# A trunk layer on one core: gate r's first two block products in the last head, a sixth pair of gate tiles, sums of tokens by eight additions

## The chip, the cores and the metric

One core of a Trainium2 chip runs the whole layer in one launch. The metric is the time of one execution in microseconds on the device; the median of several runs is what counts.

## The reference, cut to what matters

```python
u = _rmsnorm(h, norm1_g)                       # 512 tokens x 1024 channels, float32
a_glu, q, k, v, r, g_low, gate_a, gate_b = _split_cols(u @ w_in)
c = a_glu[..., :C] * sigmoid(a_glu[..., C:])
c = silu(_layernorm(_causal_dwconv(c, conv_dw_w, conv_dw_b), conv_ln_g, conv_ln_b))
y_conv = c @ w_conv_out
o = _gla_chunked(qh, kh, vh, gkh)              # 4 heads, chunks of 64 tokens
o = o * rsqrt(mean(o * o) + EPS) * gla_norm_g
y_gla = (o * silu(r)) @ w_gla_out
merged = sigmoid(gate_a) * y_conv + sigmoid(gate_b) * y_gla
h = h + merged @ w_o
u2 = _rmsnorm(h, norm2_g)
z = _causal_dwconv(u2 @ w_ffn_up, ffn_dw_w, ffn_dw_b)
h = h + (silu(z[..., :F]) * z[..., F:]) @ w_ffn_down
return _rmsnorm(h, final_g)
```

The batch is one sequence of 512 tokens; q and k have 512 columns, v, r, gate_a and gate_b have 1024 each, and F is 2816.

## The kernel before, in words

**Products.** All matrix products are held to float32 by splitting each operand into a rounded high part and the rest: three matmuls stand for one (`mm3`, lines 529 to 531: high x low, low x high, high x high). The activations are `uh`/`ul`, a weight tile (128 x 1024) is `whi`/`wlo`.

**Weights.** A list `order` fixes the sequence of the weight tiles. For each, SP issues the load into one of four `raw` buffers, ACT casts it to `whi` (line 414 or 444), and `wlo` comes in one of two ways: DVE subtracts (line 415 or 452), or, for the tiles in the set `ADDED`, ACT writes minus the weight (line 446) and POOL issues a DMA that adds the weight from memory again (line 447). There are four `whi` and four `wlo`, and a tile is prepared `LOOK` = 2 tiles ahead of its use. The program order that Python writes is each engine's order; engines wait for each other by semaphores.

**The work around the change, in PE's order.** The value weights, the convolution's inputs (`glu`), a low-rank decay, and then four heads of the linear attention, each with queries, keys, scores, states and outputs; a loop over `h` runs head `h` and the rest of head `h - 1` together, and in the gaps of a head stand `gate_b` tiles, one gate weight tile of eight k-steps and 24 matmuls of 512 columns. In the last round (h = 4) these are gate_b(2) to gate_b(5): ahead of the scores, ahead of the states, between states and outputs, and behind the outputs.

**Gate r** (`seven("w_r")`) comes next. It computes all of r with seven block products in place of eight, on 2 x 2 blocks of tokens and weights: the steps a11, a12, s1, n2, s4, n3, a22 in this order, each of two weight tiles (d = 0, 1) and 24 matmuls of 512 columns in all. a11, a12 and a22 read blocks of the activations as they are; s1, n2, s4 and n3 read sums of token blocks, which `token_sums_7` makes on DVE (passes of lines 1292 and 1305; high parts on ACT, line 1300). The weights of s1, n2 and a22 are running sums in `kept` (DVE, line 362), those of n3 are sums on POOL (line 373). Results go from PSUM banks (`x` in cv and one mm, `y` in mm, `z` in ax) to tiles `r`: `put_r` copies (ACT, line 1532), adds or subtracts (DVE, line 1539), takes the silu (ACT, line 1540) and multiplies into the head outputs `ot` (DVE, line 1546).

**Behind it** the products are transposed to channels (`gated_o`, PE line 1237, ACT line 1244, DVE line 1245), each group of four transposes into one of three ax banks: channel tiles 4 to 7 at step a22, 0 to 3 in the first pair. Then come the **pairs** of gate tiles (`pair_7`, `two_tiles`): two tiles of 1024 x 128 weights by the same seven products, here with the four weights x1, x3, x2, x4 and 84 matmuls of 256 columns, the weight sums on POOL (line 386). `MERGE` lists the pairs: gb (6, 7) and four of ga, with tiles of the output projections between and behind them. The output product w_o, the second norm, the FFN (up projection, short convolution, down projection by seven products, whose sums come from the same `token_sums_7`) and the last norm end the layer.

**Pacing.** The convolution runs on DVE as a chain of some 300 small passes (line 889), and the sums of tokens wait in a list `urgent` that is served ahead of it. Each call of `weight` hands out a share of it (`fill(share)`), so these passes are spread between the weights' own passes in DVE's order. Shares per tile are constants, as in

```python
        share = {"two": 2.5, "w_glu": RATE, "w_r": 2.0}.get(name, RATE)
        if name == "w_gb" and j > 3:
            share = 2.0 if j == 4 else 6.8
```

Of the kernel before, what the change touches and what calls it, by code (L numbers as in the profile page):

```python
# [10 lines left out]
F32 = mybir.dt.float32  # L11
# [23 lines left out]
AHEAD = 6  # L35

MERGE = [("w_gb", 6, 7), ("w_ga", 0, 1), ("w_ga", 2, 3), ("w_ga", 4, 5), ("w_ga", 6, 7)]
# [25 lines left out]
STEPS += [(step, d) for step in ("n2", "s4", "n3", "a22") for d in (0, 1)]  # L63
R_STEPS = [(step, d) for step in ("a11", "a12", "s1", "n2", "s4", "n3", "a22") for d in (0, 1)]
# [36 lines left out]
def trunk_layer(ctx: ExitStack, tc: tile.TileContext, a: dict, out: bass.AP):  # L101
# [300 lines left out]
    def split_weight(halves=False, between=None):  # L402

        if len(ready) < len(order):
# [4 lines left out]
            if name in SEVEN or name == "two":  # L409
# [5 lines left out]
                two_low[:] = [nc.vector.tensor_tensor(lo, raw, hi.bitcast(F32), ALU.subtract)]  # L415
# [54 lines left out]
    def weight(name, j, ahead=LOOK):  # L470
# [8 lines left out]
        if name == "w_gb" and j > 3:  # L479
            share = 2.0 if j == 4 else 6.8  # L480
# [783 lines left out]
    def token_sums_7(u, src, hi, lo):  # L1264
# [19 lines left out]
        def chain(step, start, *terms):  # L1284


            def one(first, op, x):
                if first:
                    work[step] = src[step]()
                begin = work[step] if not first else work[start] if isinstance(start, str) else [start]  # L1290
                for o, b, y in pieces(work[step], begin, [x]):
                    nc.vector.tensor_tensor(o, as_f32(b), f32(y), op)

            return [(1.7, lambda n=n, op=op, x=x: one(n == 0, op, x)) for n, (op, x) in enumerate(terms)]
# [75 lines left out]
    def quarters(pool, tag, bufs, halves=1, dt=F32R):  # L1370
# [11 lines left out]
        {"s1": x_src, "n2": h_src, "s4": b_src, "n3": b_src},  # L1382
# [5 lines left out]
    s1_n2, of_s1, s4, of_n2, of_s4, n3, of_n3 = merge_sums  # L1388
    heads = [Head(h) for h in range(HEADS)]
    for h in range(HEADS + 1):  # L1390
        old = heads[h - 1] if h else None
        new = heads[h] if h < HEADS else None
        if new:
            late_glu = glu(KT - LATE_GLU + h - 1) if h <= LATE_GLU else None
# [599 lines left out]
```

## Time and profile before

| | |
|---|---|
| median of 3 runs | 818.69 us (818.48 to 818.78) |
| the profiled execution | 820.03 us |
| its span in the profile | 818.3 us |
| granted clock, mean | 0.999 |
| PE busy | 808.6 us, 99% |
| DVE busy | 705.9 us, 86% |
| ACT busy | 488.9 us, 60% |
| POOL busy | 196.5 us, 24% |
| DMA | 113.60 MB, mean 139 GB/s |

How to read it. PE is TensorE, DVE is VectorE, ACT is ScalarE, POOL is GpSimd, SP issues loads. A row of a timeline gives the start, the duration, the engine, the source line, the operation, what it writes and reads, the shape, and how often it follows itself; a bracket at the end gives the engine's idle time ahead of it and what ended that. PE's matmuls overlap, so a matmul's duration is longer than the distance to the next one; the distance between starts tells what one costs. The span is what the profile covers; the execution's own time is 1.7 us longer.

### The profile page before, as it was taken

How to read it: one execution, taken by the hardware profiler on the slowest of the kernel's cores; microseconds unless marked ns; L12 is line 12 of the kernel's file. 1: busy time of each engine (PE TensorE's matmuls, PEld its weight loads, DVE VectorE, ACT ScalarE, POOL GpSimd, SP SyncE). 2: the span in 40 equal slices, each digit the busy share in tenths (PEclk: the TensorE clock that was granted, in tenths of full speed). 3: DMA queues.
4: the chain of work that ended last, by engine and by line, in shares of the span. 5: the costliest groups of instructions: out<-in, count | busy, mean ns of one | idle time of the engine just before them, and what ended most of it. 6: DMA issues, size and time to landing. Idle time of an engine off the chain costs nothing.

```text
span 818.3 us, 11468 instructions
## 1 busy us (share of the span) xinstructions
PE 808.6 (99%) x4227; PEld 695.4 (85%) x4227; DVE 705.9 (86%) x1105; ACT 488.9 (60%) x744; POOL 196.5 (24%) x176
## 2 busy tenths in 40 slices
PE   9999999999999999999999999999999999999996
PEld 8888888788888888989888898898889987899885
DVE  6879999998999878486789889989966999789895
ACT  6667788677547565394434645556445663366554
POOL 2025433332203332122001100230123311522012
PEclk9999999999999999999999999999999999999999
DMA  8488758645841232432558613156742446335662
GB/s 331 150 190 188 179 165 184 152 120 131 187 116 38 79 127 78 131 106 99 160 130 215 190 53 103 52 178 158 142 139 80 142 119 164 104 103 179 156 129 103
DMA packets 36472, 113.60 MB, mean 139 GB/s; under 512 B 3688, under 2 KB 8944, under 8 KB 36416
## 3 DMA queue, kind: packets, MB, share of 16 engines
q1 hardware_dynamic: 28912, 86.39, 30.9%
q0 software_dynamic: 7488, 26.48, 18.9%
q8 instruction: 33, 0.54, 0.3%
q14 instruction: 23, 0.19, 0.1%
q10 hardware_dynamic: 16, 0.00, 0.0%
HBM read 110.76 MB, written 2.10 MB: 138 GB/s over the span
## 4 chain that ended last, share of the span: by engine, by line
PE 85%; DVE 13%; issue 1%; ACT 1%; POOL 0%; POOLq 0%; ACTq 0%; DVEq 0%
PE mm L529 19%; PE mm L530 19%; PE mm L531 19%; DVE c L889 5%; PE cv L530 4%; PE cv L529 4%; PE cv L531 4%; DVE aside L889 3%; PE ax L531 2%; PE ax L529 2%; PE ax L530 2%; PE mm L743 2%; DVE wlo L415 1%; PE ax L1217 1%; PE cv L743 1%
## 5 line engine op out<-in xcount | busy, mean ns | idle before, releaser
L529 PE MATMUL mm<-uh,wlo 128*128 128x512 f32 (+1 forms) x532 | 193.9, 364 | 0.0
L530 PE MATMUL mm<-ul,whi 128*128 128x512 f32 (+1 forms) x532 | 191.5, 360 | 0.0
L531 PE MATMUL mm<-uh,whi 128*128 128x512 f32 (+1 forms) x532 | 191.5, 360 | 0.0
L415 DVE TENSOR_TENSOR wlo<-raw,whi 128x1024 fp32r<-128x1024 f32 x82 | 95.2, 1169 | 33.5 <-ACT whi L414 29.7
L386 POOL TENSOR_TENSOR raw<-raw,raw 128x512 f32<-128x512 f32 x39 | 60.0, 1539 | 240.1 <-DVE wlo L415 119.7
L529 PEld LDWEIGHTS mm<-uh,wlo 128*128 128x128 f32 x532 | 100.5, 189 | 15.3 <-DVE wlo L452 0.3
L531 PEld LDWEIGHTS mm<-uh,whi 128*128 128x128 f32 x532 | 100.4, 189 | 15.3
L530 PEld LDWEIGHTS mm<-ul,whi 128*128 128x128 f32 x532 | 100.5, 189 | 14.8
L414 ACT CAST whi<-raw 128x1024 fp32r<-128x1024 f32 x82 | 78.9, 966 | 39.0 <-PE mm L531 23.4
L444 ACT CAST whi<-raw 128x1024 fp32r<-128x1024 f32 x80 | 83.7, 1050 | 29.4 <-PE mm L531 13.2
L452 DVE TENSOR_TENSOR wlo<-raw,whi 128x1024 fp32r<-128x1024 f32 x50 | 66.8, 1342 | 7.4 <-ACT whi L444 7.1
L414 ACT CAST whi<-kept 128x1024 fp32r<-128x1024 f32 (+1 forms) x40 | 40.3, 1009 | 32.4 <-DVE kept L362 16.5
L415 DVE TENSOR_TENSOR wlo<-kept,whi 128x1024 fp32r<-128x1024 f32 (+1 forms) x40 | 48.8, 1221 | 7.6 <-ACT whi L414 7.5
L889 DVE SCALAR_TENSOR_TENSOR aside<-cv,pp,aside 128x255 f32<-128x255 f32 (+6 forms) x112 | 52.4, 468 | 0.0
L889 DVE SCALAR_TENSOR_TENSOR c<-aside,btmp,c 128x247 f32<-128x247 f32 (+13 forms) x93 | 52.3, 568 | 0.0
L889 DVE SCALAR_TENSOR_TENSOR c<-cv,pp,c 128x247 f32<-128x247 f32 (+13 forms) x93 | 43.4, 467 | 1.4 <-ACT c L885 1.4
L446 ACT ACTIVATE wlo<-raw 128x1024 fp32r<-128x1024 f32 x28 | 29.5, 1061 | 18.9 <-PE mm L529 18.9
L1336 ACT COPY tmp<-mm 128x256 f32<-128x256 f32 x38 | 14.1, 370 | 36.5 <-PE mm L531 35.9
L1718 DVE SCALAR_TENSOR_TENSOR tmp<-mm,pp,tmp 128x511 f32<-128x511 f32 (+1 forms) x42 | 31.0, 741 | 2.6 <-ACT tmp L1715 2.5
L1718 DVE SCALAR_TENSOR_TENSOR tmp<-tmp,pp,tmp 128x511 f32<-128x511 f32 (+1 forms) x32 | 27.8, 887 | 0.4
L1489 DVE TENSOR_TENSOR hres<-hres,mm 128x512 f32<-128x512 f32 (+1 forms) x37 | 24.6, 675 | 2.7 <-PE mm L531 1.9
L530 PE MATMUL cv<-ul,whi 128*128 128x512 f32 (+1 forms) x72 | 25.6, 356 | 0.0
(503 smaller groups left out, 2092.9 us busy)
## 6 DMA issues: line engine op xcount, KB each, us to landing
raw<-in_w_up_dram SPq DMA_DIRECT2D x44, 512.0 KB, 3.8
raw<-in_w_glu_dram SPq DMA_DIRECT2D x16, 512.0 KB, 5.0
raw<-in_w_down_dram SPq DMA_DIRECT2D x15, 512.0 KB, 4.3
wlo<-in_w_glu_dram POOLq DMA_DIRECT2D x12, 512.0 KB, 7.1
kept<-in_w_down_dram POOLq DMA_DIRECT2D x10, 512.0 KB, 6.1
raw<-in_w_v_dram SPq DMA_DIRECT2D x8, 512.0 KB, 5.4
raw<-in_w_qk_dram SPq DMA_DIRECT2D x8, 512.0 KB, 6.4
raw<-in_w_gb_dram SPq DMA_DIRECT2D x8, 512.0 KB, 4.3
```

The lines of the kernel that those rows point to most:

```text
L386: work = nc.gpsimd.tensor_tensor(out, x, y, ALU.add)
L414: nc.scalar.copy(hi, raw)
L415: two_low[:] = [nc.vector.tensor_tensor(lo, raw, hi.bitcast(F32), ALU.subtract)]
L444: nc.scalar.copy(hi, raw)
L446: pace[0] = nc.scalar.mul(lo, raw, -1.0)
L452: pace[0] = nc.vector.tensor_tensor(lo, raw, hi.bitcast(F32), ALU.subtract)
L529: nc.tensor.matmul(acc, ll, rh, start=first, stop=False, **kw)
L530: nc.tensor.matmul(acc, lh, rl, start=False, stop=False, **kw)
L531: nc.tensor.matmul(acc, lh, rh, start=False, stop=last, **kw)
L889: nc.vector.scalar_tensor_tensor(out[:, j:], x[:, : half_t - j], w, out[:, j:], ALU.mult, ALU.add)
L1489: done = nc.vector.tensor_tensor(hres[t, n][:, c], hres[t, n][:, c], acc[:, c], op)
L1718: nc.vector.scalar_tensor_tensor(z[:, s:], acc[:, : T - s], w[j], z[:, s:], ALU.mult, ALU.add)
```

## The change

Six edits go together.

1. **Sums of tokens** (`token_sums_7`) by eight additions in place of ten, through two shared sums k1 and k2. For the merge, the first three used to be computed near 31 to 39 us, and the rest in the heads; now all eight stand near the end of the last head, in `heap` buffers. The FFN's sums use the same function.
2. **Gate r** becomes a generator. Its a11 and a12 run in the last round's two slots of gate_b(4) and gate_b(5); s1 follows the heads. PSUM banks are taken when first used, and y and z change places.
3. **The low parts of a11's and a12's four weights** are made by ACT and two accumulating DMAs of POOL each, and no longer by DVE. The shares in the last round are 1.0 and 3.4 for these tiles.
4. **gate_b tiles 4 and 5** become a pair, the second of now six, behind the two w_gla tiles that follow the first, with no tile between its parts.
5. **Transposes**: channel tiles 4 and 5 at a22, then two behind each of x1, x3 and x2 of the first pair. Silu and product of two token tiles (from a12) move to n2.
6. **The FFN's list** of sums is regrouped for the eight additions.

The diff, cut to what the text speaks of:

```diff
 GROUPS = (((0, 2), (1, 3), (4, 6), (5, 7)), ((8, 10), (9, 11), (20, 21)), ((12, 14), (13, 15), (16, 18), (17, 19)))
-AHEAD = 6
-
-MERGE = [("w_gb", 6, 7), ("w_ga", 0, 1), ("w_ga", 2, 3), ("w_ga", 4, 5), ("w_ga", 6, 7)]
+AHEAD = 4
+
+MERGE = [("w_gb", 6, 7), ("w_gb", 4, 5), ("w_ga", 0, 1), ("w_ga", 2, 3), ("w_ga", 4, 5), ("w_ga", 6, 7)]
 R_PAIRS = ((0, 4), (1, 5), (2, 6), (3, 7))
 LATE_GLU = 2
 _HALVES = [("w_gla", 2 + h // 2, h % 2) for h in range(8)]
-BEHIND = [[], _HALVES[:4], _HALVES[4:8]]
+BEHIND = [[], [], _HALVES[:4], _HALVES[4:8]]
 BEHIND += [[("w_conv", m, half) for m in pair for half in range(2)] for pair in O_PAIRS[:2]]
 MERGE_REST = [("w_conv", m) for pair in O_PAIRS[2:] for m in pair]
-PLAIN_GLA = {0: (0, 1), 2: (6, 7)}
+PLAIN_GLA = {0: (0, 1), 3: (6, 7)}
 LOOK = 2
...
 STEPS = [("a11", 0), ("a11", 1), ("a12", 0), ("s1", 0), ("a12", 1), ("s1", 1)]
 STEPS += [(step, d) for step in ("n2", "s4", "n3", "a22") for d in (0, 1)]
+R_EARLY = {("a11", 0): 1.0, ("a11", 1): 1.0, ("a12", 0): 3.4, ("a12", 1): 3.4}
+R_ADDED = {("a11", 0), ("a11", 1), ("a12", 0), ("a12", 1)}
 R_STEPS = [(step, d) for step in ("a11", "a12", "s1", "n2", "s4", "n3", "a22") for d in (0, 1)]
 START = {ET.PE, ET.Activation, ET.DVE, ET.SP}
...
+                if name == "w_r" and spec[1:] in R_ADDED:
+                    two_low[:] = [nc.scalar.mul(lo, raw, -1.0)]
+                    src = block(name, spec[0], spec[2], *R_LOADS[spec[1]])
+                    for m in (slice(0, 2), slice(2, 4)):
+                        nc.gpsimd.dma_start(shaped(name, lo)[:, m], src[:, m], accum_op=ALU.add)
+                else:
+                    two_low[:] = [nc.vector.tensor_tensor(lo, raw, hi.bitcast(F32), ALU.subtract)]
                 with ExitStack() as order_of:
                     for ins in behind:
                         order_of.enter_context(tc.issue_after(ins.ins))
...
-            share = 2.0 if j == 4 else 6.8
+        if name == "w_r" and j[1:] in R_EARLY:
+            share = R_EARLY[j[1:]]
 
         fill(share + (1.75 if order[min(len(ready), len(order)) - 1] in ADDED else 0))
...
-
-
-            def one(first, op, x):
...
-
-            return [(1.7, lambda n=n, op=op, x=x: one(n == 0, op, x)) for n, (op, x) in enumerate(terms)]
+        def combine(step, l, op, r, over=None):
+
+            def at(x):
+                return work[x] if isinstance(x, str) else [x]
+
+            def one():
+                if step not in work:
+                    work[step] = work[over] if over else src[step]()
+                for o, x, y in pieces(work[step], at(l), at(r)):
+                    nc.vector.tensor_tensor(o, as_f32(x), as_f32(y), op)
...
         acts7 = {s: [[y[:, k, :] for k in range(4)] for y in x] for s, x in (("a11", a11), ("a12", a12), ("a22", a22))}
-        s1 = chain("s1", a21[0], (sub, a22[0]), (add, a21[1]), (sub, a22[1]))
-        n2 = chain("n2", "s1", (sub, a11[0]), (sub, a11[1]))
-        s4 = chain("s4", "n2", (add, a12[0]), (add, a12[1]))
-        n3 = chain("n3", a11[0], (sub, a21[0]), (add, a11[1]), (sub, a21[1]))
-        return acts7, [s1 + n2, split_sum("s1"), s4, split_sum("n2"), split_sum("s4"), n3, split_sum("n3")]
+        both = combine("k1", a11[0], add, a11[1]) + combine("k2", a21[0], add, a21[1])
+        n3 = combine("n3", "k1", sub, "k2")
+        s1 = combine("s1", "k2", sub, a22[0], "k2") + combine("s1", "s1", sub, a22[1])
+        n2 = combine("n2", "s1", sub, "k1", "k1")
+        s4 = combine("s4", "n2", add, a12[0]) + combine("s4", "s4", add, a12[1])
+        return acts7, [both + n3 + s1, split_sum("s1"), n2 + split_sum("n2"), s4 + split_sum("s4"), split_sum("n3")]
...
         {"s1": h_room, "n2": h_room, "s4": late_room, "n3": h_room},
     )
 
 
-    s1_n2, of_s1, s4, of_n2, of_s4, n3, of_n3 = merge_sums
...
-        bank = {"x": [mm_bank(), mm_bank()], "y": [mm_bank(), mm_bank()], "z": [ax_bank(), ax_bank()]}
+        y, z = (ax_bank, mm_bank) if name == "w_r" else (mm_bank, ax_bank)
+        take = {"x": mm_bank, "y": y, "z": z}
+        bank = {}
...
     rt, gated = {}, []
-    urgent += s4 + of_s4 + n3 + of_n3
-
     def sums_for(step):
         while urgent and step in ("s1", "n2", "s4", "n3") and step not in merge_acts:
             urgent.pop(0)[1]()
 
+    def multiply(t, n):
+        if (t, n) not in ((2, 0), (3, 0)):
+            nc.scalar.activation(rt[t, n], rt[t, n], AF.Silu)
+        nc.vector.tensor_tensor(ot[t, n], ot[t, n], rt[t, n], ALU.mult)
+
+    def multiply_all(done):
+        with tc.issue_after(done.ins) if done else ExitStack():
+            while gated:
+                multiply(*gated.pop(0))
+
     def put_r(step, t, n, acc):
         if step in ("a11", "s1", "n2"):
-            rt[t, n] = rp_.tile([P, T], F32, tag="r", name=nm("r"), bufs=6)
-            return nc.scalar.copy(rt[t, n], acc)
+            rt[t, n] = heap() if step == "a11" else rp_.tile([P, T], F32, tag="r", name=nm("r"), bufs=6)
+            done = nc.scalar.copy(rt[t, n], acc)
+            if step == "n2":
+                multiply_all(done)
+            return done
         if step == "a22":
             rt[t, n] = rp_.tile([P, T], F32, tag="r", name=nm("r"), bufs=6)
             nc.scalar.activation(rt[t, n], acc, AF.Silu)
...
-            nc.scalar.activation(r, r, AF.Silu)
         if step == "a22":
             done = None
-        with tc.issue_after(done.ins) if done else ExitStack():
-            while gated:
-                i, j = gated.pop()
-                nc.vector.tensor_tensor(ot[i, j], ot[i, j], rt[i, j], ALU.mult)
+        if step != "a12":
+            multiply_all(done)
         gated.append((t, n))
         if (step, t, n) == ("a22", 3, 0):
-            i, j = gated.pop()
-            nc.vector.tensor_tensor(ot[i, j], ot[i, j], rt[i, j], ALU.mult)
+            multiply(*gated.pop())
         return done if step == "n3" else None
 
     def r_at(step, i):
         if (step, i) == ("a22", 1):
-            for m in range(4, KT):
+            for m in range(4, 6):
...
+    r_work = seven("w_r", R_PAIRS, [ByTile(k) for k in range(4)], None, r_at, put=put_r, before=sums_for)
+    heads = [Head(h) for h in range(HEADS)]
+    for h in range(HEADS + 1):
+        old = heads[h - 1] if h else None
+        new = heads[h] if h < HEADS else None
+        if new:
+            late_glu = glu(KT - LATE_GLU + h - 1) if h <= LATE_GLU else None
+            new.decays()
+            new.queries()
+        else:
+            gate_b(2)
+        if old:
+            old.scores()
+        if not new:
+            urgent += n3_s1 + of_s1 + of_n2
+        new.keys() if new else gate_b(3)
+        if old:
+            old.states()
+            next(late_glu) if h <= LATE_GLU else gate_b(0) if new else next(r_work)
+            old.outputs()
+            next(late_glu) if h <= LATE_GLU else gate_b(1) if new else next(r_work)
+    behind += [roots_at[0]]
+    gla_scope.close()
+    late_scope, late = scoped("late", 1, "right")
+    r_scope, rp_ = scoped("r", 8, "right")
+    urgent += of_s4 + of_n3
+    for _ in r_work:
+        pass
     half_of = [range(KT // 2), range(KT // 2, KT)]
...
-            if n == 0 and j in (1, 2):
-                for m in range(2 * j - 2, 2 * j):
+            if n == 0 and j < 3:
+                for m in ((6, 7), (0, 1), (2, 3))[j]:
                     gated_o(m, ax_bank)
                 if j == 2:
                     start_norms()
-            if j == 0 or n >= 2:
+            if j == 0 or n >= 3:
...
             up_acts, sums = ffn_sums()
-            s1_n2, of_s1, s4, of_n2, of_s4, n3, of_n3 = sums
-            sums = [s1_n2, of_n2 + of_s1, s4 + n3, of_n3 + of_s4]
+            n3_s1, of_s1, of_n2, of_s4, of_n3 = sums
+            sums = [n3_s1[:3], n3_s1[3:] + of_n2[:1], of_n2[1:] + of_n3 + of_s1, of_s4]
```

What moves, as each engine's rows in program order. First **DVE in gate r**, the rows up to the low part of s4's second weight (the last row). Before; `kept` rows are running sums of weights, L1539 and L1546 drain r:

```order
L362 TENSOR_TENSOR kept_2078<-kept_2078,raw_2434 128x1024
L415 TENSOR_TENSOR wlo_2493<-kept_2153,whi_2492 128x1024
L1539 TENSOR_TENSOR r_2466<-ax_2428,r_2466 128x512
L362 TENSOR_TENSOR kept_2153<-kept_2153,raw_2446 128x1024
L1539 TENSOR_TENSOR r_2480<-ax_2429,r_2480 128x512
L1546 TENSOR_TENSOR h_1617<-h_1617,r_2466 128x512
L415 TENSOR_TENSOR wlo_2529<-kept_2078,whi_2528 128x1024
L362 TENSOR_TENSOR kept_2078<-kept_2078,kept_2582 128x1024
L415 TENSOR_TENSOR wlo_2538<-kept_2153,whi_2537 128x1024
L362 TENSOR_TENSOR kept_2153<-kept_2153,rx_2590 128x1024
L415 TENSOR_TENSOR wlo_2579<-raw_2434,whi_2578 128x1024
L415 TENSOR_TENSOR wlo_2587<-raw_2446,whi_2586 128x1024
```

And now (line numbers are up by 8; L1314 are low parts of token sums, L1538 drains, L1231 belongs to a head's norm):

```order
L1538 TENSOR_TENSOR h_2340<-cv_2411,h_2340 128x512
L1314 TENSOR_TENSOR sumsq_2469<-tmpq_2453,sumsq_2466 128x512
L1314 TENSOR_TENSOR sumsq_2469<-tmpq_2454,sumsq_2466 128x512
L1538 TENSOR_TENSOR h_2354<-mm_2412,h_2354 128x512
L423 TENSOR_TENSOR wlo_2448<-kept_1947,whi_2447 128x1024
L423 TENSOR_TENSOR wlo_2459<-kept_2019,whi_2458 128x1024
L1314 TENSOR_TENSOR hq_2511<-hq_2264,sumsq_2508 128x512
L1314 TENSOR_TENSOR hq_2512<-hq_2265,sumsq_2508 128x512
L364 TENSOR_TENSOR kept_1947<-kept_1947,kept_2506 128x1024
L423 TENSOR_TENSOR wlo_2503<-raw_2312,whi_2502 128x1024
L364 TENSOR_TENSOR kept_2019<-kept_2019,rx_2519 128x1024
L423 TENSOR_TENSOR wlo_2516<-raw_2322,whi_2515 128x1024
```

The twelve rows held five wlo (the first of s1, then n2 and s4), four `kept` sums and three passes on r and h. Now they hold the four wlo of n2 and s4, two `kept` sums, the two drains of a12 and four low parts of token sums; s1's wlo and the other `kept` sums stand ahead of them, and the product on h stands behind.

Second, **POOL's queue over the last head and gate r**. Before: one accumulating DMA for each gate tile, two tiny norm operations (rstd), then the weight sums of n3:

```order
L447 DMA wlo_2149<-in_w_gb_dram 128x1024
L447 DMA wlo_2194<-in_w_gb_dram 128x1024
L581 TENSOR_TENSOR rstd_2138<-mean_2136,mhalf 128x4
L447 DMA wlo_2252<-in_w_gb_dram 128x1024
L581 TENSOR_TENSOR rstd_2365<-mean_2363,mhalf 128x4
L373 TENSOR_TENSOR raw_2312<-raw_2312,raw_2434 128x512 x2
L373 TENSOR_TENSOR raw_2375<-raw_2375,raw_2446 128x512 x2
```

And now; `wlo_2249` is a11's second weight, `wlo_2307` and `wlo_2317` are a12's:

```order
L455 DMA wlo_2149<-in_w_gb_dram 128x1024
L421 DMA wlo_2194<-in_w_r_dram 128x2x256 x2
L589 TENSOR_TENSOR rstd_2138<-mean_2136,mhalf 128x4
L421 DMA wlo_2249<-in_w_r_dram 128x2x256 x2
L421 DMA wlo_2307<-in_w_r_dram 128x2x256 x2
L421 DMA wlo_2317<-in_w_r_dram 128x2x256 x2
L589 TENSOR_TENSOR rstd_2376<-mean_2374,mhalf 128x4
L375 TENSOR_TENSOR raw_2199<-raw_2199,raw_2312 128x512 x2
L375 TENSOR_TENSOR raw_2254<-raw_2254,raw_2322 128x512 x2
```

gate_b(4) and gate_b(5) had one issue each; r's four weights have two each, three of them between the two rstd.

Third, **PE at the end of a22**: the last transpose of the third group, eight matmuls of the first pair, and the fourth group (`ax_2769`), before:

```order
L1237 MATMUL ax_2760<-ident,h_2146 128x128
L529 MATMUL mm_2782<-uh_97,wlo_2703 128x256
L530 MATMUL mm_2782<-ul_98,whi_2702 128x256
L531 MATMUL mm_2782<-uh_97,whi_2702 128x256
L529 MATMUL mm_2782<-uh_97,wlo_2703 128x256
L530 MATMUL mm_2782<-ul_98,whi_2702 128x256
L531 MATMUL mm_2782<-uh_97,whi_2702 128x256
L529 MATMUL mm_2782<-uh_97,wlo_2703 128x256
L530 MATMUL mm_2782<-ul_98,whi_2702 128x256
L1237 MATMUL ax_2769<-ident,h_2140 128x128
L1237 MATMUL ax_2769<-ident,h_2142 128x128
L1237 MATMUL ax_2769<-ident,h_2144 128x128
```

And now, from the last two transposes of the second group on:

```order
L1245 MATMUL ax_2691<-ident,h_2144 128x128
L1245 MATMUL ax_2691<-ident,h_2146 128x128
L537 MATMUL mm_2704<-uh_97,wlo_2642 128x256
L538 MATMUL mm_2704<-ul_98,whi_2641 128x256
L539 MATMUL mm_2704<-uh_97,whi_2641 128x256
L537 MATMUL mm_2704<-uh_97,wlo_2642 128x256
L538 MATMUL mm_2704<-ul_98,whi_2641 128x256
L539 MATMUL mm_2704<-uh_97,whi_2641 128x256
L537 MATMUL mm_2704<-uh_97,wlo_2642 128x256
```

Two groups of transposes stand ahead of the first pair's x1, and x1's matmuls follow each other; the next two groups come behind all of x1.

More of the change, by code (lines that the diff above doesn't have):

```diff
@@ L1282, in as_f32 @@
             return x if x.dtype == F32 else f32(x)
-        def chain(step, start, *terms):
-            def one(first, op, x):
[L1288 to L1292, printed above, removed]
-            return [(1.7, lambda n=n, op=op, x=x: one(n == 0, op, x)) for n, (op, x) in enumerate(terms)]
+        def combine(step, l, op, r, over=None):
[6 more added lines that the diff above has]
+                    nc.vector.tensor_tensor(o, as_f32(x), as_f32(y), op)
+            return [(1.7, one)]
         def split_sum(step):
@@ L1483, in seven @@
             half, n, op, whole = into[step]
+            if of[step] not in bank:
+                bank[of[step]] = [take[of[step]]() for _ in range(2)]
             for i in range(2):
```

49 lines of the change are left out of this document (14 added, 35 removed).

## The prediction

> **What bounds the kernel now.** I read the page first: the busy times, then the clock.
>
> ```profile
> span 818.3 us, 11468 instructions
> PE 808.6 (99%) x4227; PEld 695.4 (85%) x4227; DVE 705.9 (86%) x1105; ACT 488.9 (60%) x744; POOL 196.5 (24%) x176
> PEclk9999999999999999999999999999999999999999
> ```
>
> TensorE (PE) is busy 99% of the span at full clock, so the time changes only if PE gets fewer or shorter matmuls, or if its few waits come or go. VectorE (DVE) at 86% is second, but an average hides stages. So I read the windows around the change: last head (222 to 247), gate r (247 to 286), and the 82 us ahead of them.
>
> ```profile
> core 0: us, PE busy (x) PEld busy (x) DVE busy (x) ACT busy (x) POOL busy (x), PEclk, DMA share, GB/s
> 140.00:222.00 82.00, 81.83 (x377) 67.52 (x376) 78.53 (x190) 55.99 (x105) 24.18 (x23) 1.00 0.66 155
> 222.00:247.00 25.00, 25.00 (x118) 21.02 (x117) 24.43 (x40) 14.07 (x30) 2.32 (x2) 1.00 0.40 106
> 247.00:269.00 22.00, 22.00 (x99) 18.23 (x98) 19.89 (x18) 15.00 (x21) 8.15 (x4) 1.00 0.15 50
> 269.00:286.00 17.00, 16.71 (x79) 13.61 (x78) 15.22 (x17) 9.74 (x13) 7.53 (x4) 1.00 0.18 59
> ```
>
> In the last head PE has no free time to fill (25.00 of 25.00): gate_b(4) and gate_b(5) fill it already. DVE is full too, 24.43 of 25. So DVE is the engine that this change can bring onto the path. PE's only waits near the change are in the timeline of its matmuls (the DVE row is used in part 2):
>
> ```profile
> 278.86 0.39 PE L531 MATMUL mm<-whi,sumsq 128*128 128x512 f32 x1
> 279.53 0.47 PE L529 MATMUL cv<-whi,ul 128*128 128x512 f32 x1 [0.29 <-DVE r L1539]
> ...
> 276.48 2.31 DVE L415 TENSOR_TENSOR wlo<-kept,whi 128x1024 fp32r<-128x1024 f32 x1
> ...
> 287.24 0.28 PE L530 MATMUL mm<-ul,whi 128*128 128x256 f32 x1
> 288.22 0.66 PE L1237 MATMUL ax<-ident,h 128*128 128x128 f32 x4 [0.71 <-DVE h L1245]
> ```
>
> **Part 1: two gate tiles become a pair.** PE issues its matmuls at a fixed distance, read from starts of steps: 24 matmuls of 512 columns from 246.44 to 251.88, and 24 of 256 columns from 310.92 to 313.80.
>
> ```profile
> 246.44 0.39 PE L529 MATMUL cv<-whi,ul 128*128 128x512 f32 x1
> 251.88 0.39 PE L529 MATMUL ax<-whi,ul 128*128 128x512 f32 x1
> ...
> 310.92 0.28 PE L529 MATMUL mm<-uh,wlo 128*128 128x256 f32 x1
> 313.80 0.40 PE L529 MATMUL mm<-oa,wlo 128*128 128x512 f32 x1
> ```
>
> That is 5.44/24 = 0.2267 us and 2.88/24 = 0.120 us. Two plain tiles are 48 x 0.2267 = 10.88 us; a pair is 7 products of 12, 84 x 0.120 = 10.08 us. **Saved: 0.80 us**, if the pair's weights are on time. It has no tile behind it, so four weights must be made in 10 us; the pair's sums on POOL are off PE's path as in the five pairs of before, which run without a wait apart from the transposes above.
>
> [...]
>
> **Part 2: the two waits that go.** Against the spacing, 279.53 comes 0.67 after its predecessor instead of 0.2267: 0.44 lost. This is a22 waiting for its bank: the subtraction (r) that empties it stood on DVE behind the wlo of 276.48, which took 2.31, twice its usual length, beside a POOL pass. In the new order a wlo stands ahead of it too, but POOL's passes for the next pair come later: they need two loads that take the buffers which n3's wlo set free. At 288.22, the matmul comes 0.98 after its predecessor instead of 0.12: 0.86 lost. There a fourth group of transposes wants one of three banks, which DVE and ACT are still emptying. The new order puts two groups at each place, so there is always a bank. **Saved: 0.44 + 0.86 = 1.30 us**; at worst half of it, if two groups ahead of x1 still meet a full bank.
>
> **Part 3: gate r comes 10.88 us earlier, and DVE must follow.** a11 and a12 move into the last head; s1 then starts where a11 started. What DVE must have done by then is what counts. Before, it was ahead only by this:
>
> ```profile
> 268.20 0.39 PE L529 MATMUL mm<-whi,sumsq 128*128 128x512 f32 x1
> 269.79 0.39 PE L530 MATMUL mm<-wlo,sumsq 128*128 128x512 f32 x1
> ...
> 264.68 2.35 DVE L415 TENSOR_TENSOR wlo<-raw,whi 128x1024 fp32r<-128x1024 f32 x2
> ```
>
> The wlo of s4's second weight is done at 264.68 + 2.35 = 267.03; PE first reads it at 269.79 (the eighth matmul of s4): a margin of 2.8 us. The change takes away 10.88 of time and also takes work from DVE ahead of this point. Durations, start to start:
>
> ```profile
> 232.96 1.23 DVE L415 TENSOR_TENSOR wlo<-kept,whi 128x1024 fp32r<-128x1024 f32 x1 [0.28 <-ACT whi L414]
> 234.10 0.48 DVE L1206 SCALAR_TENSOR_TENSOR state<-state,dec,ax 128x256 f32<-128x256 f32 x1
> ...
> 236.09 1.29 DVE L1292 TENSOR_TENSOR tmpq<-hq,uh 128x512 f32<-128x512 f32 x2
> 237.29 1.29 DVE L1292 TENSOR_TENSOR tmpq<-tmpq,ul 128x512 f32<-128x512 f32 x2
> ...
> 30.76 1.22 DVE L1292 TENSOR_TENSOR xq<-uh,uh 128x1024 f32<-128x1024 f32 x1
> 36.44 2.48 DVE L1292 TENSOR_TENSOR xq<-xq,ul 128x1024 f32<-128x1024 f32 x2
> 44.46 0.69 DVE L967 TENSOR_TENSOR h<-mm,tmp 128x512 f32<-128x512 f32 x1 [5.54 <-PE mm L531]
> ```
>
> A wlo is 1.14, a 128x512 pass 0.60. Four wlo (a11, a12) go to ACT and POOL: -4.56. One of the three r/h passes ahead of s4 moves behind it: -0.60. The sums do not get shorter here, although they are eight and not ten: before, three of them were done at 30.76 to 38.9, where DVE idles 5.54 us right after, and only 14 half passes stood in this stretch (8.4 us). Now all eight stand here, 16 halves (9.6): +1.20. Together -3.96. Idle of DVE that the denser order could use, from 222 on (a further 0.28 is in the row above):
>
> ```profile
> 232.26 0.42 DVE L1203 COPY state<-ax 128x256 f32<-128x256 f32 x1 [0.21 <-PE ax L1199]
> 248.58 1.50 DVE L415 TENSOR_TENSOR wlo<-raw,whi 128x1024 fp32r<-128x1024 f32 x1 [0.74 <-ACT whi L414]
> ```
>
> 0.21 + 0.28 + 0.74 = 1.23. So DVE is late by 10.88 - 2.8 - 3.96 - 1.23 = **2.9 us, and PE waits for it** at n2 and s4. I take 2.9. The upper end is 4.1, where none of the idle is recovered.
>
> Four sums of weights on POOL run beside DVE in this stretch; beside it such a pass takes 2.04, alone (at 321.31, two in 2.68) 1.34.
>
> ```profile
> 247.14 4.08 POOL L373 TENSOR_TENSOR raw<-raw,raw 128x512 f32<-128x512 f32 x2 [2.21 <-DMA raw<-in_w_r_dram]
> 253.62 4.07 POOL L373 TENSOR_TENSOR raw<-raw,raw 128x512 f32<-128x512 f32 x2 [2.39 <-ACT whi L414]
> 321.31 2.68 POOL L386 TENSOR_TENSOR raw<-raw,raw 128x512 f32<-128x512 f32 x2 [12.36 <-DVE wlo L415]
> ...
> 250.00 1.78 DVE L1305 TENSOR_TENSOR hq<-tmpq,sumsq 128x512 fp32r<-128x512 f32 x1
> 254.22 2.32 DVE L415 TENSOR_TENSOR wlo<-kept,whi 128x1024 fp32r<-128x1024 f32 x1
> 257.06 1.71 DVE L362 TENSOR_TENSOR kept<-kept,raw 128x1024 f32<-128x1024 f32 x1
> ```
>
> DVE pays for it: 1.78 for one half pass (0.69 = 1.29 - 0.60 elsewhere), 2.32, 1.71 and 1.50 (at 248.58) for 1024 columns (1.23 at 232.96), together 1.09 + 1.09 + 0.48 + 0.27 = 2.9 us. Both kernels have these four passes. If they now fall where DVE waits for something else, this cost goes, and the wait with it (2.9 - 2.9 = 0); that is the lower end. I keep 2.9, since a DVE that is late has no waits for them to fall into.
>
> [...] The rows lie between sharing and blocking: both engines were slowed.
>
> **Costed at nothing, and why.** The new route of the four wlo: on ACT two more multiplications than before, in a window where it is 14.07 of 25 busy. On POOL eight issues in place of two, ahead of an rstd:
>
> ```profile
> 223.55 0.92 POOL L447 DMA_DIRECT2D wlo<-in_w_gb_dram  x1 [2.96 <-ACT wlo L446]
> 243.54 1.40 POOL L581 TENSOR_TENSOR rstd<-mean,mhalf 128x4 f32<-128x4 f32 x1 [19.07 <-DVE mean L1223]
> DMA to landing us min/median/max: 5.4/8.9/11.8
> 231.40 0.60 ACT L1252 ACTIVATE h<-mm 128x512 f32<-128x512 f32 x1 [3.98 <-PE mm L531]
> 240.79 0.58 PE L529 MATMUL mm<-uh,wlo 128*128 128x512 f32 x1
> ```
>
> POOL is idle 19 us there. The landing is the tight point. a12's second wlo can be begun when gate_b(3) has freed its buffer (231.4), so its issues fall near 233.7, and it lands at 239 to 245.5. PE reads it 1.6 after 240.79, at 242.4. So 0 to 3.1; I take 0, as the transfers are half as long as those in the row, and as any wait there gives DVE the same time: the two waits do not add, the longer counts. The same holds for the state copies, which now stand between sums. Removing 20% of the sums in the FFN removes DVE work beside which PE has no gap: nothing. The silu and products moved to n2 leave DVE's total as it is.
>
> **The sum.** -0.80 - 1.30 + 2.9 = +0.8 us on a span of 818.3: 819.1. The profiled execution took 820.03, so 1.7 lies around the span, and it is 1.3 above the median of 818.69; the change goes onto the median: **819.5**. A measurement of this kernel can tell about 0.2% (1.64 us) from no change: faster is below 817.05, slower above 820.33.
>
> **Rivals.**
> - *No new wait* (0.20). DVE gets ahead in the 82 us before the last head, where it idles 82.00 - 78.53 = 3.5 us: if the order there, with two tiles' paced work moved, recovers most of it, or if POOL's passes cost DVE nothing, the wait is 0 to 0.4, and 818.69 - 2.1 = 816.6 stands. For it: the idle and the cost are there. Against: the convolution works on PE's results, which do not come earlier.
> - *DVE's idle is not recovered* (0.28, slower). The 0.74 at 248.58 is a wait for ACT's cast, and such casts stand ahead of every wlo; then the wait is 4.1 and the sum +2.0: 820.7. It decides from a wait of 3.74 on. The chain behind it makes it worse: the second load of the next pair waits for the last wlo of n3, POOL adds and ACT casts, and the last products that the transposes need stand behind that cast; by the same durations this is just level with PE, and up to 1 us more gives 821.7.
> - *POOL's sums and DVE's passes exclude each other* (0.03): in the denser order all four meet a pass, DVE waits them out, the wait is 5.4 and the sum +3.3: 822.0. Against: both engines' rows above were slowed, neither stood still.
> [...]
>
> **How the numbers follow.** The forecast has 0.46, with a wait of 0.5 to 3.7: 817.1 to 820.3, all of it "same". So faster 0.20, same 0.46, slower 0.28 + 0.03 + 0.03 = 0.34. The range runs from 816.6 (no wait) to 821.6 (the slower rival to near its end); outside lie the last two rivals, the end of the second and what of the first goes lower, 2 in 10.
>
> **What would show it.** Right: no wait at a22's first matmul and none in the transposes; a pair of gb in 10.1 us; a wait of PE for DVE (wlo, or a sum) in gate r ahead of n2 or s4, 0.5 to 3.7 us in all; DVE in that stretch without idle. Wrong: PE waits in the last head for an accumulated wlo; PE waits at the lone pair for weights; no wait of PE in gate r; or a wait anywhere in the FFN that was not there before.

## The result, and the profile after

The changed kernel takes **834.13 us** (831.64 to 834.84), before 818.74 in the same runs: ratio 1.0182, 95% interval 1.0169 to 1.0195. The forecast was 819.5 us, with a range of 816.6 to 821.6 and the largest single chance (0.46) on no measurable change. The time lies 12.5 us above the range.

The page of the profile after, the same lines as those shown of before:

```profile
span 833.1 us, 11567 instructions
PE 812.1 (97%) x4263; PEld 698.7 (84%) x4263; DVE 697.1 (84%) x1105; ACT 491.9 (59%) x752; POOL 209.9 (25%) x186
PEclk9999999999997999999999999999999999999998
```

PE is still the busiest, but one digit of its clock is a 7 (and the last an 8), where before every one was a 9. The 7 is the thirteenth slice of forty, 250 to 271 us. The windows view says the same in time:

```profile
core 0: us, PE busy (x) PEld busy (x) DVE busy (x) ACT busy (x) POOL busy (x), PEclk, DMA share, GB/s
247.00:269.00 22.00, 13.35 (x48) 10.52 (x47) 11.78 (x16) 7.36 (x13) 7.33 (x7) 0.77 0.21 41
```

PE is busy 13.35 of 22 us where it was busy all 22, and DVE, which the prediction had feared, is idle for half of it. Who is waited for stands in PE's timeline after (L537 to L539 are the three products):

```profile
233.92 0.40 PE L537 MATMUL mm<-whi,ul 128*128 128x512 f32 x1
236.39 0.47 PE L538 MATMUL mm<-wlo,uh 128*128 128x512 f32 x1 [2.07 <-DMA wlo<-in_w_r_dram]
...
237.62 0.57 PE L537 MATMUL mm<-whi,ul 128*128 128x512 f32 x1
241.27 0.39 PE L537 MATMUL mm<-whi,ul 128*128 128x512 f32 x1
...
245.75 0.47 PE L538 MATMUL cv<-wlo,uh 128*128 128x512 f32 x1 [0.38 <-DMA wlo<-in_w_r_dram]
246.98 0.40 PE L537 MATMUL cv<-whi,ul 128*128 128x512 f32 x1
256.03 0.76 PE L538 MATMUL cv<-wlo,uh 128*128 128x512 f32 x1 [8.65 <-DMA wlo<-in_w_r_dram]
256.59 0.63 PE L539 MATMUL cv<-whi,uh 128*128 128x512 f32 x1
257.01 0.63 PE L537 MATMUL cv<-whi,ul 128*128 128x512 f32 x1
261.65 0.39 PE L539 MATMUL mm<-whi,uh 128*128 128x512 f32 x1
```

Three times PE waits for a weight whose low part is made by accumulating DMAs: a11's second (236.39), a12's first (245.75) and a12's second (256.03). Against the spacing of 0.2267 us these cost 2.24 + 0.72 + 8.82 = 11.8 us. Behind the first and the third, matmuls start 0.43 us apart and not 0.2267: nine from 237.62 to 241.27 take 3.65 in place of 2.04, thirteen from 256.03 to 261.65 take 5.62 in place of 2.95, another 4.3 us. The sum of 16.1, less the gains of the pair (0.8) and of the transposes (0.9), is 14.4; the span grew by 833.1 - 818.3 = 14.8.

POOL's queue shows where the low parts were held up:

```profile
230.99 1.06 ACT L418 ACTIVATE wlo<-raw 128x1024 fp32r<-128x1024 f32 x1 [0.41 <-PE mm L537]
...
226.83 1.23 POOL L421 DMA_DIRECT2D wlo<-in_w_r_dram  x1 [2.99 <-ACT wlo L418]
...
245.94 1.19 POOL L421 DMA_DIRECT2D wlo<-in_w_r_dram  x1 [3.32 <-ACT junk L1229]
251.26 1.22 POOL L421 DMA_DIRECT2D wlo<-in_w_r_dram  x1 [4.13 <-issue]
...
DMA to landing us min/median/max: 4.2/4.6/5.2
```

ACT had done its part of the last weight by 232.1 (the first row), but POOL issues the last six DMAs from 226.83 to 251.26, 4.5 to 5.3 us apart, each about when the one before it has landed (4.2 to 5.2 us). "issue" is time in which the profile shows nothing that was waited for.

### The profile page after: what moved, and what is told of

Its sections match the earlier page's. It is cut to its first block, busy times and chain, and to the rows that moved or that the text cites. A ratio compares the mean times of both kernels' runs of the same rounds, so it can differ in the third digit from the quotient of the medians.

```text
span 833.1 us, 11567 instructions
## 1 busy us (share of the span) xinstructions
PE 812.1 (97%) x4263; PEld 698.7 (84%) x4263; DVE 697.1 (84%) x1105; ACT 491.9 (59%) x752; POOL 209.9 (25%) x186
## 4 chain that ended last, share of the span: by engine, by line
PE 78%; DVE 14%; issue 3%; DMA 2%; ACT 2%; POOL 1%; POOLq 0%; ACTq 0%; DVEq 0%
PE mm L537 18%; PE mm L538 18%; PE mm L539 18%; DVE c L897 5%; PE cv L538 4%; PE cv L539 4%; PE cv L537 4%; DVE aside L897 3%; PE ax L539 2%; PE ax L538 2%; PE ax L537 2%; PE mm L751 2%; DVE wlo L423 1%; DMA wlo<-in_w_r_dram 1%; DMA kept<-in_w_down_dram 1%
## 5 line engine op out<-in xcount | busy, mean ns | idle before, releaser
L537 PE MATMUL mm<-uh,wlo 128*128 128x512 f32 (+1 forms) x536 | 194.6, 363 | 0.0
L539 PE MATMUL mm<-uh,whi 128*128 128x512 f32 (+1 forms) x536 | 192.5, 359 | 0.0
L388 POOL TENSOR_TENSOR raw<-raw,raw 128x512 f32<-128x512 f32 x42 | 66.8, 1590 | 248.6 <-DVE wlo L423 159.9
L539 PEld LDWEIGHTS mm<-uh,whi 128*128 128x128 f32 x536 | 101.2, 189 | 15.4
L537 PEld LDWEIGHTS mm<-uh,wlo 128*128 128x128 f32 x536 | 101.3, 189 | 14.8
L423 DVE TENSOR_TENSOR wlo<-kept,whi 128x1024 fp32r<-128x1024 f32 (+1 forms) x38 | 45.2, 1193 | 7.3 <-ACT whi L416 7.2
L1742 DVE SCALAR_TENSOR_TENSOR tmp<-mm,pp,tmp 128x511 f32<-128x511 f32 (+1 forms) x48 | 35.5, 742 | 3.7 <-ACT tmp L1739 3.7
L454 ACT ACTIVATE wlo<-raw 128x1024 fp32r<-128x1024 f32 x26 | 27.3, 1058 | 15.1 <-PE mm L537 15.1
L388 POOL TENSOR_TENSOR raw<-raw 128x512 f32<-128x512 f32 x14 | 25.8, 1842 | 0.0
```

Source lines behind the costliest of these rows:

```text
L388: work = nc.gpsimd.tensor_tensor(out, x, y, ALU.add)
L454: pace[0] = nc.scalar.mul(lo, raw, -1.0)
L537: nc.tensor.matmul(acc, ll, rh, start=first, stop=False, **kw)
L539: nc.tensor.matmul(acc, lh, rh, start=False, stop=last, **kw)
L1742: nc.vector.scalar_tensor_tensor(z[:, s:], acc[:, : T - s], w[j], z[:, s:], ALU.mult, ALU.add)
```

## The experiments

Two theories for the slow issues. **Room**: the memory that the kernel reserves for the descriptors of POOL's DMAs (`dynamic_dma_scratch_size=1024`) is short, a DMA of 128x2x256 fills more than half of it, and so the next one waits until it is empty. **Writing**: POOL simply needs 5 us to write the descriptors of 256 runs of 1 KB. Of the next four kernels, e1_room and e3_four tell the two apart; e2_dve and e4_rows take the slow issues away, to show what is left of the prediction once the weights are on time. The kernel before had 819.0 us beside these four.

**e1_room**

```diff
-    nc = _bacc.Bacc("TRN2", ..., dynamic_dma_scratch_size=1024)
+    nc = _bacc.Bacc("TRN2", ..., dynamic_dma_scratch_size=2048)
```

> The changed kernel with the memory for POOL's DMA descriptors doubled, from 1024 to 2048 bytes per partition; nothing else. Theory room: the eight accumulating DMAs of w_r were issued 4.5 to 5.5 us apart because a DMA of 128x2x256 (256 runs of 1 KB) fills the room for descriptors, so that the next one waits until the last has landed (4.2 to 5.2 us). Then with twice the room two or more are under way at once, the issues come in pairs or threes 1.2 us apart, PE's waits of 2.2, 0.7 and 8.8 us in the last head shrink to at most 3 us together, and the time is 817 to 824 us. Theory writing: POOL needs about 5 us to write 256 descriptors, whatever the room. Then nothing changes: issues 4.5 to 5.5 us apart, 831 to 835 us.

821.34 us; ratio to before 1.0027 (1.0018 to 1.0037), so 12.8 us of the 15.4 are gone. POOL's queue in this run:

```profile
223.46 3.70 POOL L421 DMA_DIRECT2D wlo<-in_w_r_dram  x3 [2.94 <-ACT wlo L418]
228.19 1.20 POOL L421 DMA_DIRECT2D wlo<-in_w_r_dram  x1 [1.04 <-issue]
```

Three go out 1.23 us apart, the fourth waits 1.04. PE waits for no DMA any more. The room decides: an issue that does not wait takes 1.20 to 1.23 us.

**e2_dve**

```diff
-R_ADDED = {("a11", 0), ("a11", 1), ("a12", 0), ("a12", 1)}
+R_ADDED = set()
```

> The changed kernel with part 3 of the change undone alone: the low parts of the four early r weights are made by DVE again, no accumulating DMA. Both theories of the slow issues: PE's waits for the accumulating DMAs go. The theory of the prediction (DVE becomes the bound of gate r): DVE has 4.56 us more to do than in the changed kernel, so PE waits 2.9 + 4.6 = 7.5 us for it in the last head and gate r, and the time is about 818.7 - 2.1 + 7.5 = 824 us. Rival (DVE has slack that the sum did not see): 817 to 820 us.

827.23 us; ratio 1.0100 (1.0086 to 1.0114). PE now waits for DVE, at n2, s4, n3 and a22:

```profile
253.57 0.50 PE L538 MATMUL mm<-wlo,hq 128*128 128x512 f32 x1 [0.28 <-DVE wlo L423]
259.91 0.50 PE L538 MATMUL ax<-wlo,sumsq 128*128 128x512 f32 x1 [1.92 <-DVE wlo L423]
266.93 0.50 PE L538 MATMUL mm<-wlo,sumsq 128*128 128x512 f32 x1 [0.91 <-DVE wlo L423]
276.06 0.77 PE L537 MATMUL mm<-whi,ul 128*128 128x512 f32 x1 [3.62 <-DVE r L1538]
276.62 0.63 PE L538 MATMUL mm<-wlo,uh 128*128 128x512 f32 x1
282.08 0.39 PE L539 MATMUL mm<-whi,uh 128*128 128x512 f32 x1
```

Against the spacing the four waits cost 7.4 us in all, and the sum had 7.5. The places differ: 2.5 us fall at n2 and s4, where the prediction had its wait, 1.1 at n3 and 3.8 at a22's first matmul. The time is 3 us above the expected 824. In the profiled execution (827.79 us, granted clock 0.993) behind the wait of 3.62 stands half speed again: thirteen matmuls from 276.62 to 282.08 take 5.46 in place of 2.95, or 2.5 more. But two of the four executions, with a granted clock of 0.997, took 826.7 us, only 1 us less; what makes up the rest of the 3 us is not shown. With DVE making these weights, gate r's early start costs more than the change brings.

**e3_four**

```diff
-                    for m in (slice(0, 2), slice(2, 4)):
+                    for m in (slice(0, 1), slice(1, 2), slice(2, 3), slice(3, 4)):
```

> The changed kernel with each low part accumulated by four DMAs of 128x256 in place of two of 128x2x256: the same bytes and the same 1 KB runs, half as many in each DMA. Theory room: two or three of the smaller DMAs are under way at once, so a weight is through in about half the time; PE's wait of 8.8 us falls below 5 and the time is 820 to 828 us. Theory writing: as many descriptors and two more DMAs for each weight; not faster, 832 to 838 us.

822.22 us; ratio 1.0039 (1.0025 to 1.0053). Twice as many DMAs of half the size, in the old room, are nearly as good as the larger room: against "writing" once more. At most three go out in a row, then there is a wait:

```profile
223.45 2.69 POOL L421 DMA_DIRECT2D wlo<-in_w_r_dram  x3 [2.96 <-ACT wlo L418]
226.92 0.88 POOL L421 DMA_DIRECT2D wlo<-in_w_r_dram  x1 [0.79 <-issue]
...
244.84 0.47 PE L538 MATMUL cv<-wlo,uh 128*128 128x512 f32 x1 [2.54 <-issue]
```

The counts in the changed kernel, e1_room and e3_four fit one size of the room, if it is counted in runs of contiguous bytes: one DMA of 256 runs at a time in 1024 bytes, three but not four of 256 in 2048, three but not four of 128 in 1024. By that 1024 bytes hold 384 to 511 runs and 2048 bytes 768 to 1023. This is an estimate from these three counts; how a run is kept in the room, nothing here shows.

**e4_rows**

```diff
-                    src = block(name, spec[0], spec[2], *R_LOADS[spec[1]])
-                    for m in (slice(0, 2), slice(2, 4)):
-                        nc.gpsimd.dma_start(shaped(name, lo)[:, m], src[:, m], accum_op=ALU.add)
+                    nc.gpsimd.dma_start(lo, a["w_r_rows"][2 * (spec[1] == "a12") + spec[2]], accum_op=ALU.add)
```

> The changed kernel with the source of the accumulating DMAs laid out in rows of 4 KB (a second copy of the four blocks in memory), one DMA of 128x1024 for each weight as the gate tiles have; loads and everything else as in the changed kernel. Both theories of the slow issues: an issue costs 0.9 us as for gate tiles, and PE does not wait for these weights by more than 1 us. Then what the prediction said of DVE can be seen: its forecast is a wait of 2.9 us for DVE at n2 and s4 and 819.5 us (817.1 to 820.3); its first rival no new wait and 816.6 us. If instead the 1 KB runs are not the cause: 830 us or more.

821.04 us; ratio 1.0024 (1.0014 to 1.0034). The four DMAs are issued in 0.84 to 0.92 us without a wait, and PE waits for none. What remains is what the prediction was about:

```profile
252.21 0.50 PE L536 MATMUL mm<-wlo,hq 128*128 128x512 f32 x1 [0.29 <-DVE wlo L421]
254.44 0.50 PE L536 MATMUL mm<-wlo,hq 128*128 128x512 f32 x1 [0.56 <-DVE wlo L421]
259.02 0.50 PE L536 MATMUL ax<-wlo,sumsq 128*128 128x512 f32 x1 [0.20 <-DVE wlo L421]
261.29 0.50 PE L536 MATMUL ax<-wlo,sumsq 128*128 128x512 f32 x1 [0.61 <-DVE wlo L421]
271.71 0.47 PE L535 MATMUL mm<-whi,ul 128*128 128x512 f32 x1 [0.85 <-DVE r L1536]
...
249.79 1.29 POOL L375 TENSOR_TENSOR raw<-raw,raw 128x512 f32<-128x512 f32 x1
250.32 1.83 DVE L421 TENSOR_TENSOR wlo<-kept,whi 128x1024 fp32r<-128x1024 f32 x1 [1.05 <-ACT whi L416]
251.04 2.27 POOL L375 TENSOR_TENSOR raw<-raw,raw 128x512 f32<-128x512 f32 x1
252.08 2.31 DVE L421 TENSOR_TENSOR wlo<-kept,whi 128x1024 fp32r<-128x1024 f32 x1
253.27 2.27 POOL L375 TENSOR_TENSOR raw<-raw,raw 128x512 f32<-128x512 f32 x1
254.31 1.78 DVE L1312 TENSOR_TENSOR hq<-hq,sumsq 128x512 fp32r<-128x512 f32 x1
```

PE waits for DVE at n2 (L536 reading `hq`) and s4 (reading `sumsq`), 0.29 + 0.56 + 0.20 + 0.61 = 1.66 us of idle time, or 2.3 us against the spacing, and 0.85 (1.0) at a22's first matmul. The last six rows are the last three of POOL's four weight sums and n2's two wlo with a half pass behind them, one by one. They take turns. The sum at 249.79 was there first and takes 1.29, no longer than alone (1.34 at 321.31 in the profile before); the wlo at 250.32 ends 1.07 after it, and 1.23 is what it takes alone, so it did next to nothing until the sum was through. The next sum begins at 251.04 and ends 1.16 after that wlo, and so on to the half pass. Together the three passes of DVE take 5.92 us in place of 3.15 (1.23, 1.23 and 0.69 alone): 2.8 lost.

**e5_dmasum** takes these sums from POOL's arithmetic:

```diff
-                for c in (slice(0, T), slice(T, D)):
-                    nc.gpsimd.tensor_tensor(b12[:, c], b12[:, c], b22[:, c], ALU.add)
+                nc.gpsimd.dma_start(kept[pairs, d, "b12"], a["w_r_rows"][4 + d], accum_op=ALU.add)
```

> e4_rows with POOL's four weight sums of n3 (7.8 us beside DVE from 247.8 on) replaced by two accumulating DMAs from rows of 4 KB; the sums are the same. Theory contention: the remaining waits of PE for DVE in e4_rows (about 1.7 us at n2 and s4 and 0.85 at a22's first matmul) come from POOL's passes slowing DVE's (2.9 us by the profile of before); without them the waits fall below 0.7 us together and the time is 1.5 to 2.5 us less than e4_rows: 818.5 to 819.5, beside 819.0 for before, or less. Rival, DVE is simply late by the earlier start of s1: waits as in e4_rows and 820.5 to 821.5 us.

819.33 us beside 818.9; ratio 1.0002 (0.9993 to 1.0011). The waits at n2 and s4 are gone, all four; the one at a22 is left:

```profile
248.09 1.81 POOL L373 DMA_DIRECT2D raw<-in_w_r_rows_dram  x2
250.69 1.23 DVE L419 TENSOR_TENSOR wlo<-kept,whi 128x1024 fp32r<-128x1024 f32 x1 [1.06 <-ACT whi L414]
252.16 1.23 DVE L419 TENSOR_TENSOR wlo<-kept,whi 128x1024 fp32r<-128x1024 f32 x1 [0.24 <-ACT whi L414]
...
262.61 3.52 POOL L386 TENSOR_TENSOR raw<-raw,raw 128x512 f32<-128x512 f32 x2 [12.71 <-DVE wlo L419]
266.09 1.74 POOL L386 TENSOR_TENSOR raw<-raw 128x512 f32<-128x512 f32 x1
266.61 2.31 DVE L419 TENSOR_TENSOR wlo<-kept,whi 128x1024 fp32r<-128x1024 f32 x1
269.66 0.47 PE L533 MATMUL mm<-whi,ul 128*128 128x512 f32 x1 [0.88 <-DVE r L1534]
```

So the waits at n2 and s4 need POOL's passes beside DVE's (contention); the work that DVE has to do does not bring them by itself. The wait at a22 looks like a second such place: POOL's third pass for the first pair runs from 266.09 to 267.83, and the wlo of a22 that begins at 266.61 takes 2.31, ending 1.09 after it.

**e6_plain**

```diff
-MERGE = [("w_gb", 6, 7), ("w_gb", 4, 5), ("w_ga", 0, 1), ...]
+MERGE = [("w_gb", 6, 7), ("w_ga", 0, 1), ...]
...
+        if n == 0:
+            gate_b(4)
+            gate_b(5)
```

> e5_dmasum with the sixth pair undone: gate_b(4) and gate_b(5) as two plain tiles behind the two w_gla tiles. By the spacing of matmuls (0.2267 and 0.120 us) the pair saves 0.80 us, so this is 0.8 us slower than e5_dmasum. Rival: the pair's four weights without a tile behind it are not ready in 10 us, and this is as fast or faster.

819.36 us; ratio to before 1.0005 (0.9996 to 1.0013). By the time there is no difference to e5_dmasum (819.33): the 0.8 us expected did not show. PE's timeline has the pair's gain all the same. In e5_dmasum the pair begins and the next pair follows at

```profile
300.52 0.28 PE L533 MATMUL mm<-uh,wlo 128*128 128x256 f32 x1
310.59 0.28 PE L533 MATMUL cv<-uh,wlo 128*128 128x256 f32 x1
```

10.07 us later; in e6_plain the two plain tiles stand from

```profile
299.85 0.39 PE L535 MATMUL mm<-uh,wlo 128*128 128x512 f32 x1
310.76 0.28 PE L535 MATMUL mm<-uh,wlo 128*128 128x256 f32 x1
```

10.91 us. PE gives 0.4 of the 0.84 back ahead of the pair: the first half of the first w_gla tile takes 3.15 us up to the second half in e5_dmasum (from 288.71 on) and 2.74 in e6_plain (from 288.48 on). At the next pair e5_dmasum is still 0.17 ahead (310.59 against 310.76), but its span ends 0.4 later (817.8 against 817.4); where that goes stays open, and differences of this size are within what these runs can tell.

**e7_trans**

```diff
-            for m in range(4, KT):
+            for m in range(4, 6):
                 gated_o(m, ax_bank)
...
-            if n == 0 and j in (1, 2):
-                for m in range(2 * j - 2, 2 * j):
+            if n == 0 and j < 3:
+                for m in ((6, 7), (0, 1), (2, 3))[j]:
```

> The kernel before with only the transposes spread (two channel tiles at a22, two behind each of x1, x3, x2). The prediction gave this -0.86 us: PE's wait at the fourth group goes and nothing takes its place, 818.1 beside 819.0. Rival: the product tiles or the cast of x3 come later and the wait reappears in another place, no change or slower.

818.01 us beside 818.9; ratio 0.9995 (0.9986 to 1.0004): the medians differ by the forecast 0.9, the interval does not exclude no change. PE's timeline has no wait at the transposes, and here none at a22 either.

**e8_layout**

```diff
-        "w_r": _cols(w_in, tiles(C_R, KT)),
+        "w_r": _r_rows(_cols(w_in, tiles(C_R, KT))),
```

> e5_dmasum without a second copy: w_r lies in memory only in rows of 4 KB, in the order of the blocks, so that SP's loads of r also have 4 KB runs (1 KB before). If only the accumulating DMAs were short of room, this is the same as e5_dmasum within 0.5 us; if SP's loads of 1 KB runs cost something too, up to 1 us faster.

818.84 us beside 818.9; ratio 1.0001 (0.9992 to 1.0010), 0.5 below e5_dmasum, a difference too small to tell by the two intervals. All weights of r lie in rows of 4 KB. This is the change with its fault mended and without POOL's four sums, and it is level with the kernel before.

**e9_later and e10_both** try to remove the second place of contention:

```diff
+                if name == "two" and spec == ("w_gb", 6, 7, "x1"):
+                    third.append(raw_tile())
+                    with tc.issue_after(two_low[0].ins):
+                        nc.vector.memset(third[0][:, :1], 0.0)
                 nc.scalar.copy(hi, raw)
```

> e8_layout with the first pair's weight sums on POOL held back until DVE is through with a22's weights (a one-column fill by DVE of the buffer that they write). In e8_layout PE waits 0.9 us for r at a22's first matmul, because the wlo ahead of r on DVE takes 2.31 us beside a POOL pass. Theory contention: that wlo takes 1.2 us, the wait goes, and the time is 0.9 us less than e8_layout. Rival: the sums come too late and PE waits at the first pair's second weight instead; no gain or slower.

> The same hold on POOL's sums in e7_trans (the kernel before with only the transposes spread). In e7_trans the wait at a22 was not there in the profiled run (POOL's passes had ended just before the wlo), so no change is expected: within 0.3 us of e7_trans; if in its other runs the two collide, up to 0.5 us less.

Both are slower: 821.66 us, ratio 1.0027 (1.0016 to 1.0038), and 821.41 us, ratio 1.0020 (1.0011 to 1.0029), beside 819.57. In e9_later the wlo takes 1.21 and a22 waits no more, but POOL's sums begin at 270.14, ACT's cast of them comes later, DVE stands 2.26 us for it at 275.08, and the drain of the transposes behind that on DVE is late. PE waits at the second group of transposes:

```profile
265.33 1.21 DVE L423 TENSOR_TENSOR wlo<-kept,whi 128x1024 fp32r<-128x1024 f32 x1
270.14 3.83 POOL L385 TENSOR_TENSOR raw<-raw,raw 128x512 f32<-128x512 f32 x2 [20.36 <-ACT r L1517]
275.08 1.23 DVE L423 TENSOR_TENSOR wlo<-raw,whi 128x1024 fp32r<-128x1024 f32 x1 [2.26 <-ACT whi L417]
280.45 1.11 PE L1245 MATMUL ax<-ident,h 128*128 128x128 f32 x4 [2.18 <-DVE h L1253]
281.58 0.41 PE L538 MATMUL mm<-hq,whi 128*128 128x256 f32 x1
283.68 0.28 PE L539 MATMUL mm<-hq,whi 128*128 128x256 f32 x1
```

The contention theory holds for the wlo and for a22. For the time the rival holds, though the wait is at the transposes and not, as it said, at the first pair's second weight. Behind the wait ten matmuls of 256 columns, from 281.58 to 283.68, take 2.10 us in place of 1.20. e10_both, where nothing was expected, has the same wait of 2.18 us at its transposes; in its profiled execution (820.18 us, granted clock 0.998) no slow matmuls follow. Six of its eleven executions took 821.4 us or more, at 0.996; no trace of one of those is kept.

## Why the prediction was wrong, point by point

- **The failing step** is in "Costed at nothing": "its issues fall near 233.7, and it lands at 239 to 245.5 ... So 0 to 3.1; I take 0". Waiting for the accumulated weights was the right place to look, but the term was mis-sized: it measured 11.8 us of waits (8.8 of them at a12's second weight, the only one that the prediction weighed), and 4.3 us of half speed behind them, which was no term of the sum. The last issue was at 251.26 and not 233.7. I had taken the issue cost from a row of another shape (0.92 us for 128x1024 in rows of 4 KB) and bounded only the landing, which was indeed shorter (4.2 to 5.2 us). The eight DMAs of 128x2x256 in one queue had no row in the trace of before, and what they share, the room for descriptors, was not among the bounds; e1_room shows that it was the cause: with twice the room the issues are 1.23 us apart and PE waits for none of these DMAs. The argument "POOL is idle 19 us there" looked at POOL's arithmetic and not at the resource that its DMAs use.
- **That the two waits do not add** held: with DVE given that time, the changed kernel has no wait for a wlo of DVE at n2 or s4.
- **DVE late by 2.9 us** was right in place, once the weights are on time: 2.3 us by the spacing in e4_rows, at n2 and s4. e2_dve agrees with the sum in total (7.4 against 7.5), but with 2.5 of it at n2 and s4. e5_dmasum shows that the wait stands and falls with POOL's passes: without them it is gone, which was the lower end.
- **The rival that POOL's sums and DVE's passes exclude each other** had a chance of 0.03, since "both engines' rows above were slowed, neither stood still". That reading came from rows that merge two passes. Taken one by one, the passes of e4_rows take turns (POOL's sums 1.29, 2.27 and 2.27 us, DVE's wlo 1.83 and 2.31). So the rival was right in kind there and its price wrong: DVE lost 2.8 us and not 4 x 1.34 = 5.4, four sums at their length alone, because not every sum held up a pass of DVE for its whole length (the one at 249.79 did for its last 0.76 us).
- **The pair, 0.80 us**: right on PE (10.07 against 10.91), not found in the time. The second 0.03 in the chance of slower stood for a pair that costs more than two plain tiles; no run shows such a loss: on PE the pair took 0.84 us less, and the times are level (819.33 and 819.36).
- **The transposes, 0.86 us**: right in the profiles, where the wait is gone with the new places but for the two kernels that hold POOL's sums back; e7_trans has the 0.9 in its median, with an interval that does not exclude no change.
- **a22's wait, 0.44 us, would go**: wrong. It was 0.40 after by the spacing and 1.04 in e5_dmasum. The reason given, that POOL's passes for the pair come later, failed: they began at 262.61 in e5_dmasum and their third, at 266.09, stood beside the same wlo. That gate r and the loads moved together is the likely reason, and not shown.
- **The sum without the fault** was +0.8 us; e4_rows measured 821.04 - 819.0 = +2.0, e8_layout without POOL's sums nothing. So even with the weights on time this kernel is slower than before by more than the noise (1.0014 to 1.0034), though its time is inside the range. One weakness is in the start of the sum: the 1.30 us of part 2 were read in an execution of 820.03 us and taken off a median that is 1.3 lower. Whether a median execution has those two waits, no trace shows.

## What to carry to other kernels

In these runs an accumulating DMA of POOL holds a part of a shared room for descriptors until about when it lands (issues 4.5 to 5.3 us apart beside landings of 4.2 to 5.2; with twice the room three in a row, 1.23 apart): count the runs of contiguous bytes of all that are under way at once, and where a new one has shorter runs than those in the trace, treat its queue as unknown and not its landing alone. Rows that merge several instructions show a mean: take them apart before you say how two engines share (2.04 us for each of POOL's sums before; 1.29, 2.27 and 2.27 one by one in e4_rows). When work moves from a busy engine to an idle one, ask what besides the engine's time the new route uses. And a wait of PE is worth more than its length where matmuls run slower behind it (4.3 us more behind waits of 11.8 in the changed kernel).

## What the runs showed of the hardware that was not expected

- POOL issued a DMA of 256 runs of 1 KB every 4.5 to 5.3 us with 1024 bytes for descriptors, and every 1.23 us, three at a time, with 2048.
- Matmuls of 512 columns start about 0.43 us apart, and not 0.2267, behind some waits: in the changed kernel for 3.6 us after a wait of 2.07 (from 1.2 us after it on) and 5.6 us after 8.65, in e2_dve for 5.5 us after 3.62. The wait of 2.54 in e3_four had no such tail. Two waits of the same 2.18 us, in e9_later and e10_both, had one with a tail and one without. That a wait of 2.07 is enough and one of 2.54 is not, and that 2.18 can go either way, means that the length alone does not decide; what does, no run here shows.
- Where DVE's passes and POOL's sums overlapped in e4_rows, they took turns: POOL's took 1.29 (first there), 2.27 and 2.27 us and DVE's wlo 1.83 and 2.31, against 1.34 and 1.23 alone. The mean of such rows looks like sharing (2.04 for POOL's sums before). The chain on DVE that is level with PE showed the loss at once: PE waits 2.3 us at n2 and s4 in e4_rows, and not there in e5_dmasum.
